# Attention stage of a two-layer streaming encoder: key pairs on column halves, scores in one burst, tile halves fixed by hand, opening in half products

## The chip, the cores and the metric

The kernel runs on one core of a Trainium2 chip, in fp32 and in fp32r (fp32 split into a high and a low part, so that one product is three matmuls: high by high, high by low, low by high). The metric is the time of one execution on the device in microseconds (us). The kernel before takes 2203.91 us, the median of three runs that lie between 2200.82 and 2206.71.

## The reference

One step of a two-layer encoder over 2048 prompt tokens and 32 sample tokens, with a model width of 1024. Layer one is a gated DeltaNet (projections, short convolution, a recurrence in blocks of 64, a gate, an output projection, LayerNorm). From its result `h` a shared K and V are projected, and layer two is attention over a window of the query's own chunk of 64 keys and the two chunks before it, with 16 query heads on 4 key heads of 64 and a learned sink for each head. The change lies in layer two:

```python
def sink_softmax(s, sinks):
    sk = sinks.astype(jnp.float32)[..., None, None]
    m = jnp.maximum(s.max(-1, keepdims=True), sk)
    p = jnp.exp(s - m)
    return p / (p.sum(-1, keepdims=True) + jnp.exp(sk - m))
...
    q = rope_partial(proj[..., :B_QW].reshape(b, l, B_Q_HEADS, B_HD), pos) * (B_HD ** -0.5)
    z = proj[..., B_QW:]
    o = cached_attention(q, k, v, sk) if cached else banded_attention(q, k, v, sk)
    out = (o * jax.nn.silu(z)) @ w_out
    return layer_norm(DN_ALPHA * x + out, ln_g, ln_b)
```

The prompt is 32 chunks of 64 tokens. Chunk n sees the keys of chunks n-2, n-1 and n, 192 keys (chunk 0 sees 64, chunk 1 sees 128). The 32 sample tokens see 128 cached keys and their own 32.

## The kernel before, in words

**Stages.** `P1` projects q, k, v and the gate of layer one; `Delta` runs the recurrence; `O1` makes the output projection and LayerNorm of layer one; `P2` projects V, K, Q and Z of layer two from `h`; `Attention` makes scores, softmax, values, the gate, the output projection and LayerNorm of layer two.

**P2.** Tokens are taken in blocks of 416. Block 0 (phase 0) is projected plainly: a unit is a kind (v, k, q or z) and a number j, it is 256 output columns, and it takes four products (`plain`, L1319). One product is 12 matmuls of 128x416 (L1291 to L1293). The other blocks go in two pairs (phases 1 and 2) by a Winograd scheme of seven products a unit (`winograd`, L1336) on sums of the inputs, which `load_pair` (L1205) makes on VectorE (DVE in the profile) and ScalarE (ACT). The weights of a product are one piece of 512 KB; a ring of 12 pieces holds them, and each product calls for the next loads on ACT's DMA queue (`load`, L1266). After each product up to two pieces of finishing work are taken from a list (`after`, L1304): for q and k a rotation of four DVE operations (`rope`, L1420), for z a tanh on ACT and one DVE operation (`gate`, L1400), for v four transposes and two ACT copies (`turn`, L1406). `sequence` (L1737) sets the order of the units: z0, z1, z2 of phase 0; ten units of phase 1; z3, k0, q0 of phase 0; ten units of phase 2; q1, q2, q3, v0 of phase 0. Six products of the first group lie in stage O1, six beside `load_pair(1)` (L1758); the twelve of z3, k0, q0 lie beside `load_pair(2)` (L1763). The last sixteen products lie in the attention stage, four ahead of each of the chunks 10 to 13 (L1772 to L1776).

**Attention.** Chunks go in the order 10 to 31, then 0 to 9, then the sample. `chunk(n)` (L1610) does two head pairs p, one after the other, and each is a chain of steps: four fp32 score matmuls of 64 rows into `S` (L1624), row maxima on DVE (L1499), four exponentials with row sums on ACT (L1507), one over the sum on DVE (L1510, L1511), scaling of `P` on GpSimd (POOL, L1632), six transposes (L1639) in two groups of three, whose results ACT (L1641) and DVE (L1643) copy, three fp32 value matmuls of 128 rows by 128 columns and 256 moving columns into `ot` (L1645), and the gate (L1648). For the value matmul each chunk of 64 keys stands twice in `vd`, in a block-diagonal form: 128 rows hold the keys for two heads, half of every block is zero. An fp32 matmul is two MATMUL records in the trace, a transpose is one.

Two finished chunks make a tile of 128 tokens. `finish` (L1514) makes its output projection: two halves of 512 columns of 24 matmuls each (L1532 to L1534), then the residual, the statistics (L1535 to L1538), `rsqrt_power` on POOL (L466, L468), the scaling by ACT and POOL (L1543 to L1545) and the store (L1553). There are 17 tiles, the sample's among them. The output weights are 16 pieces of 512 KB, loaded by SP's queue (L999) once P2's memory is free (`open_right`, L1466).

**What sets the order.** Stages before attention are under `manual_schedule`: the order of PE, DVE and ACT is the order of the code. The attention stage is not: there the compiler's planner orders all engines by a simulated time. The queues of SP and POOL are ordered by the planner in both kernels.

Of the kernel before, what the change touches and what calls it, by code (L numbers as in the profile page):

```python
# [19 lines left out]
D = 1024  # L20
NP = 2048
# [1113 lines left out]
class P2:  # L1135
# [10 lines left out]
    def __init__(self, tc, right, mid, I, O, T, G):  # L1146
        self.tc, self.nc, self.I, self.O, self.T, self.G = tc, tc.nc, I, O, T, G
        self.res = new_pool(tc, right, "p2_res", 1, side="right")
        self.wp = new_pool(tc, right, "p2_w", self.RING, side="right")
# [3 lines left out]
        self.ppl = None  # L1153
        self.turn = 0
        self.todo, self.second, self.staged = [], [], []
# [110 lines left out]
    def load(self, most=2):  # L1266

        for _ in range(most):
            if self.loads and len(self.held) < self.RING:
                what, slot = self.loads.pop(0)  # L1270
                w = self.wp.tile([128, 2, 4, 128], F32R, tag="w", name="w")
                src = self.T["w2"][UNITS.index(what[:2]), SLOTS.index(slot)]
                self.nc.scalar.dma_start(w[:].rearrange("p s k c -> p s (k c)").bitcast(F32), src)
# [13 lines left out]
    def product(self, ps, w, x, first, last):  # L1287
        nc = self.nc
        for k in range(4):
# [5 lines left out]
    def units(self, units):  # L1295

        self.loads = [(u, s) for u in units for s in self.slots(u)]
        self.held = []
# [20 lines left out]
    def plain(self, unit):  # L1319
# [3 lines left out]
        for c in range(2):  # L1323
            ps = (self.ppl or self.ppr).tile([128, 512], F32, tag="ps", name="ps")[:, :TB]
            for h in range(2):
                self.product(ps, self.weight(unit, self.PLAIN[c][h]), x[4 * h:4 * h + 4], h == 0, h == 1)
# [111 lines left out]
class Attention:  # L1438


    def __init__(self, tc, left, I, O, T, G):
# [6 lines left out]
        self.ps_s = [new_pool(tc, left, "t_ps", 1, PSUM, side=L)]  # L1448
        self.ps_t = new_pool(tc, left, "t_pt", 2, PSUM, side=L)
        self.ps_o = new_pool(tc, left, "t_po", 1, PSUM, side=L)  # L1450
        self.turn = 0
        self.kT = one.tile([128, 2, NP], F32, tag="kT", name="kT")

        self.vd = one.tile([128, 32, 2, 128], F32, tag="vd", name="vd")
        self.nsk = one.tile([128, 8], F32, tag="nsk", name="nsk")
# [7 lines left out]
        self.pend = []  # L1463
        self.data = {}

    def open_right(self, right):  # L1466
        tc, I = self.tc, self.I
        R = "right"
        self.oone = new_pool(tc, right, "u_one", 1, side=R)
        self.otwo = new_pool(tc, right, "u_two", 2, side=R)  # L1470
        self.pp = new_pool(tc, right, "u_pp", 1, PSUM, side=R)
        self.ps_s.append(new_pool(tc, right, "u_ps", 1, PSUM, side=R))
        rest = load_out_weights(self.nc, self.oone, self.T["wo"][1], self.nc.sync)
        self.w = next(rest)
        drain(rest)

    def tables(self):
        self.tabs = ln_tables(self.nc, self.oone, self.I["b_ln_g"], self.I["b_ln_b"])

    def load_kv(self, a, z):  # L1480
        nc, T = self.nc, self.T
        nc.sync.dma_start(self.kT[:, :, a * 64:z * 64], T["bk"][:, :, a * 64:z * 64].rearrange("a p t -> p a t"))
# [7 lines left out]
    def scores_tile(self):  # L1490
        self.turn += 1
        return self.ps_s[self.turn % len(self.ps_s)].tile([128, 2, 2, 256], F32, tag="S", name="S")

    def softmax(self, S, P, nskc):

        nc, V, thr = self.nc, self.nc.vector, self.thr
        nsub = len(P)
        nm = thr.tile([128, 4], F32, tag="nm", name="nm")
        V.tensor_reduce(out=nm[:, :nsub], in_=S, axis=AX.X, op=ALU.max, negate=True)  # L1499
        V.tensor_tensor(out=nm[:, :nsub], in0=nm[:, :nsub], in1=nskc, op=ALU.min)  # L1500
        sm = thr.tile([128, 4], F32, tag="sm", name="sm")
        es_ = thr.tile([128, 4], F32, tag="es", name="es")
        for u in range(nsub):
            src = S[:, u, :]
            if len(P[u].shape) == 3:
                src = src.rearrange("r (j k) -> r j k", k=64)
            nc.scalar.activation(P[u], src, AF.Exp, bias=nm[:, u:u + 1], scale=1.0, accum_out=sm[:, u:u + 1])  # L1507
        V.tensor_tensor(out=es_[:, :nsub], in0=nm[:, :nsub], in1=nskc, op=ALU.subtract)
        nc.scalar.activation(es_[:, :nsub], es_[:, :nsub], AF.Exp)
        V.tensor_tensor(out=sm[:, :nsub], in0=sm[:, :nsub], in1=es_[:, :nsub], op=ALU.add)  # L1510
        V.reciprocal(out=sm[:, :nsub], in_=sm[:, :nsub])  # L1511
        return sm

    def finish(self, t0, n, graw, late=False, tail=False):  # L1514
        nc, V, pool = self.nc, self.nc.vector, self.otwo
# [5 lines left out]
        nc.gpsimd.tensor_tensor(out=glo[:, :, :n], in0=graw[:, :, :n], in1=ghi[:, :, :n], op=ALU.subtract)  # L1521
        st = pool.tile([128, 2, 6], F32, tag="st", name="st")
        w, tabs = self.w, self.tabs
        both = self.scores_tile() if late else None
        for c in range(2):
            cs = slice(c * 512, c * 512 + 512)
            if late:
# [3 lines left out]
            for k in range(KC):  # L1531
                nc.tensor.matmul(ps[:n], ghi[:, k, :n], w[0][k][:, cs], start=(k == 0), stop=False)  # L1532
                nc.tensor.matmul(ps[:n], ghi[:, k, :n], w[1][k][:, cs], start=False, stop=False)  # L1533
                nc.tensor.matmul(ps[:n], glo[:, k, :n], w[0][k][:, cs], start=False, stop=(k == KC - 1))  # L1534
            V.scalar_tensor_tensor(out=r[:n, cs], in0=r[:n, cs], scalar=ALPHA, in1=ps[:n], op0=ALU.mult, op1=ALU.add)  # L1535
            V.bn_stats(out=st[:n, c, :], in_=r[:n, cs])
# [399 lines left out]
```

## Time and profile before

| what | value |
|---|---|
| median of three runs | 2203.91 us |
| the profiled execution's own time | 2203.02 us |
| its span, first to last instruction | 2201.2 us |
| mean granted TensorE clock | 0.987 |
| DVE, ACT, POOL busy | 68%, 41%, 32% of the span |
| DMA moved | 430 MB, mean 195 GB/s |

The page gives busy times, the span in 40 slices, the DMA queues, the chain of work that ended last, and groups of instructions by line. The trace behind it can be asked for a stretch (the windows view), for instructions in order of time (the timeline view), and for waits. Matmuls are pipelined in it, so a matmul's own duration is longer than its share of TensorE's time; the time from one start to the next is what counts. An entry such as "x6 1.46" is six records whose joint stretch is 1.46 us. PEclk is the granted TensorE clock, 1.00 being full.

### The profile page before, as it was taken

The numbers are of one execution on the slowest core, as the hardware profiler recorded it, in microseconds if no ns is written. First come the engines' busy times: TensorE is split into PE (matmuls) and PEld (weight loads), VectorE is DVE, ScalarE is ACT, GpSimd is POOL, SyncE is SP. The second block draws the span as 40 slices with busy tenths as digits, with TensorE's granted clock in tenths as the row PEclk, the third lists the DMA queues.
The fourth block names the chain that finished last, engine by engine and source line by source line (L and its number), as shares of the span: only waits on it lengthen the run. The fifth ranks groups of instructions, "written<-read, shape, count | busy, mean of one in ns | idle before, by whom it ended". The sixth has DMA issues, their size and how long they took to land.

```text
span 2201.2 us, 37188 instructions
## 1 busy us (share of the span) xinstructions
PE 2103.0 (96%) x13370; PEld 1911.1 (87%) x13370; DVE 1490.1 (68%) x2771; ACT 911.1 (41%) x2405; POOL 713.5 (32%) x1176
## 2 busy tenths in 40 slices
PE   8999999999989999998889999899899988999997
PEld 6999999999989889887778888899899976888775
DVE  5888977876657589888865665555835566556663
ACT  5545545544422477667742111311311034444441
POOL 1212211161111188788841210000000025565653
PEclk9999999999999999999999999999999999999999
DMA  7656656567764645545735766888788895333321
GB/s 283 224 186 192 223 172 195 175 191 242 243 212 161 204 131 163 153 147 180 235 105 179 255 218 243 298 278 284 266 285 285 273 305 135 100 83 96 96 73 43
DMA packets 348377, 430.00 MB, mean 195 GB/s; under 512 B 78352, under 2 KB 276080, under 8 KB 348176
## 3 DMA queue, kind: packets, MB, share of 16 engines
q1 hardware_dynamic: 311856, 311.07, 44.5%
q10 hardware_dynamic: 36336, 116.55, 15.8%
q8 instruction: 106, 1.74, 0.3%
q14 instruction: 79, 0.65, 0.1%
HBM read 269.45 MB, written 158.44 MB: 194 GB/s over the span
## 4 chain that ended last, share of the span: by engine, by line
PE 77%; DVE 9%; POOL 5%; ACT 4%; DMA 3%; issue 2%; ACTq 0%; SPq 0%; POOLq 0%; DVEq 0%
PE ps L77 10%; PE ps L79 10%; PE ps L78 10%; PE ps L1291 5%; PE ps L1292 5%; PE ps L1293 5%; PE ot L1645 3%; PE po L1052 3%; PE po L1054 3%; PE po L1053 3%; PE po L1532 3%; PE po L1533 3%; PE po L1534 3%; PE S L1624 2%; POOL Tt L588 2%
## 5 line engine op out<-in xcount | busy, mean ns | idle before, releaser
L77 PE MATMUL ps<-act_hi,w_hi 128*128 128x416 f32 x1280 | 458.7, 358 | 6.4 <-DVE z L322 2.7
L79 PE MATMUL ps<-act_hi,w_lo 128*128 128x416 f32 x1280 | 450.5, 353 | 5.0 <-POOL w_lo L54 3.2
L78 PE MATMUL ps<-act_lo,w_hi 128*128 128x416 f32 x1280 | 451.3, 353 | 0.0
L77 PEld LDWEIGHTS ps<-act_hi,w_hi 128*128 128x128 f32 x1280 | 241.8, 189 | 11.0 <-DVE z L322 3.1
L79 PEld LDWEIGHTS ps<-act_hi,w_lo 128*128 128x128 f32 x1280 | 242.0, 189 | 9.8 <-POOL w_lo L54 4.3
L78 PEld LDWEIGHTS ps<-act_lo,w_hi 128*128 128x128 f32 x1280 | 242.6, 190 | 2.8
L1291 PE MATMUL ps<-xs_h,w 128*128 128x416 f32 x560 | 199.6, 356 | 11.4 <-DVE ra L1348 7.1
L1292 PE MATMUL ps<-xs_l,w 128*128 128x416 f32 x560 | 199.9, 357 | 3.1 <-DVE xs_l L1194 3.1
L1293 PE MATMUL ps<-xs_h,w 128*128 128x416 f32 x560 | 198.4, 354 | 0.0
L54 POOL TENSOR_TENSOR w_lo<-w_raw,w_hi 128x1024 fp32r<-128x1024 f32 x32 | 80.5, 2516 | 357.3 <-ACT w_hi L53 343.3
L295 DVE SCALAR_TENSOR_TENSOR y<-R,convw,y 128x2083 f32<-128x2083 f32 (+2 forms) x78 | 175.1, 2245 | 24.8 <-ACT y L293 24.6
L585 POOL TENSOR_TENSOR tm<-L,Tt 128x60 f32<-128x60 f32 (+19 forms) x375 | 136.3, 363 | 87.9 <-DVE L L572 49.9
L588 POOL TENSOR_TENSOR Tt<-Tt,tm 128x60 f32<-128x60 f32 (+19 forms) x375 | 143.6, 383 | 28.3
L1632 POOL TENSOR_TENSOR P<-P,sm 128x384 f32<-128x384 f32 (+2 forms) x128 | 100.9, 810 | 119.1 <-DVE sm L1511 56.5
L1486 POOL MEMSET vd<- 64x768 f32 (+2 forms) x10 | 7.8, 778 | 397.0 <-DVE ra L1348 396.7
L1507 ACT ACTIVATE P<-S,nm 128x192 f32<-128x192 f32 (+2 forms) x260 | 104.6, 419 | 61.1 <-DVE nm L1500 52.3
L1291 PEld LDWEIGHTS ps<-xs_h,w 128*128 128x128 f32 x560 | 106.4, 190 | 14.6 <-DVE ra L1348 7.8
L1348 DVE SCALAR_TENSOR_TENSOR ra<-ps,u 128x416 f32<-128x416 f32 x60 | 35.4, 590 | 122.3 <-PE ps L1293 121.4
L1052 PE MATMUL po<-wo,g_hi 128*128 128x512 f32 (+1 forms) x272 | 110.7, 407 | 0.9 <-DVE hT L1100 0.9
L1292 PEld LDWEIGHTS ps<-xs_l,w 128*128 128x128 f32 x560 | 106.2, 190 | 5.6 <-DVE xs_l L1194 4.2
L1293 PEld LDWEIGHTS ps<-xs_h,w 128*128 128x128 f32 x560 | 106.9, 191 | 1.2
L95 ACT CAST pre_hl<-pre_raw 128x256 fp32r<-128x256 f32 x184 | 65.7, 404 | 101.6 <-DMA pre_raw<-in_b_w_z 25.8
(298 smaller groups left out, 4799.8 us busy)
## 6 DMA issues: line engine op xcount, KB each, us to landing
w<-s_w ACTq DMA_DIRECT2D x180, 512.0 KB, 4.6
s_w<-pre_hl SPq DMA_DIRECT2D x160, 256.0 KB, 2.5
w_raw<-in_w_in SPq DMA_DIRECT2D x32, 512.0 KB, 6.5
s_wo<-pre_hl SPq DMA_DIRECT2D x64, 256.0 KB, 4.1
gb<-s_gcum SPq DMA_DIRECT2D x34, 256.0 KB, 5.2
k<-s_k SPq DMA_DIRECT2D x34, 256.0 KB, 4.0
s_z<-z SPq DMA_DIRECT2D x40, 208.0 KB, 2.1
s_q<-y SPq DMA_DIRECT2D x8, 1024.0 KB, 5.2
```

The lines of the kernel that those rows point to most:

```text
L77: nc.tensor.matmul(ps, hi[:, k, :], xh[:, k, :], start=(k == 0), stop=False)
L78: nc.tensor.matmul(ps, hi[:, k, :], xl[:, k, :], start=False, stop=False)
L79: nc.tensor.matmul(ps, lo[:, k, :], xh[:, k, :], start=False, stop=(k == KC - 1))
L295: self.nc.vector.scalar_tensor_tensor(out=y[:, a:z], in0=R[:, a + j:z + j], scalar=self.convw[:, i, j:j + 1], in1=y[:, a:z], op0=ALU.mult, ...
L585: P.tensor_tensor(out=tm[:n, i0 - k:, :w], in0=L[:n, i0:, j:j + 1].to_broadcast(sh), in1=Tt[:n, j:j + 1, :w].to_broadcast(sh), op=ALU.mult)
L588: P.tensor_tensor(out=Tt[:n, i0:, :w], in0=Tt[:n, i0:, :w], in1=tm[:n, i0 - k:, :w], op=ALU.subtract)
L1052: nc.tensor.matmul(ps[:n], ghi[:, k, :n], w[0][k][:, cs], start=(k == 0), stop=False)
L1291: nc.tensor.matmul(ps, w[:, 0, k], xh[:], start=first and k == 0, stop=False, skip_group_check=True)
L1292: nc.tensor.matmul(ps, w[:, 0, k], xl[:], start=False, stop=False, skip_group_check=True)
L1293: nc.tensor.matmul(ps, w[:, 1, k], xh[:], start=False, stop=last and k == 3, skip_group_check=True)
L1507: nc.scalar.activation(P[u], src, AF.Exp, bias=nm[:, u:u + 1], scale=1.0, accum_out=sm[:, u:u + 1])
L1632: nc.gpsimd.tensor_tensor(out=P[:, u, :nj], in0=P[:, u, :nj], in1=f.unsqueeze(1).unsqueeze(3).to_broadcast([128, nj, 2, 64]), op=ALU.mult)
```

## The change

1. **Values on column halves.** Of the three key chunks of a window, two adjoining ones are a pair of 128 keys (`keys`). For the pair, V stands as it is (`vp`, 128 keys by 256 columns, a second load of V), and each head half is a value matmul of 128 rows by 64 columns whose output goes to one half of the PSUM partitions (`ot[hs, p]`). The single chunk uses `vd` as before, one half of the columns at a time. Three fp32 matmuls of 128 columns for each head pair become four of 64 columns. The six transposes stay six.
2. **Scores in one burst.** Both head pairs' scores of a chunk are made together, and the steps of a chunk are spread over two rounds: `beside(n)` makes the scores and the softmax of chunk n, and the transposes and values of the chunk before it.
3. **Order by hand.** The attention stage is under `manual_schedule` for PE, DVE and ACT. A tile's output projection is cut into eight pieces of six matmuls, and each round takes four, so that a half tile ends just ahead of the values. The next tile's split (`ready`) comes in the fifth piece or after, the scaling of a tile (`scale`) in the third piece of the next tile.
4. **Opening in half products.** The last plain products are yielded by halves (`fine`), and `opening` puts the steps of the chunks 10 to 13 between them, chunk 10's scores after six halves.
5. **Plain products dealt out anew.** z3 goes ahead of phase 1 (ten products beside `load_pair(1)` in place of six), v0 takes z3's place beside `load_pair(2)`, and twelve products are left for the opening in place of sixteen.
6. **Output weights in the ring.** The weight ring outlives P2, and its last 12 loads are the first 12 pieces of the output weights; four are left to load after P2. LayerNorm's tables are loaded then too.
7. **The sample** goes after chunk 31 in place of last, and the last tile's store is cut in two, on two queues.

PSUM is dealt out anew: two score tiles from the start, one transpose tile at first and a second after P2.

```diff
-        for k in range(4):
+        for k in ks:
...
-        self.loads = [(u, s) for u in units for s in self.slots(u)]
+        self.loads = [(u, s) for u in units for s in self.slots(u)] + [(None, i) for i in range(self.RING)]
...
+                for ks in ((0, 1), (2, 3)) if self.fine else (range(4),):
+                    if ks[0] == 2:
+                        yield 1.13
+                    self.product(ps, w, x[4 * h:4 * h + 4], h == 0, h == 1, ks)
...
+                if pair is not None:
+                    for h in range(2):
+                        hs = slice(h * 64, h * 64 + 64)
+                        nc.tensor.matmul(ot[hs, p], self.vp[:, pair, p * 128 + h * 64:p * 128 + h * 64 + 64],
+                                         pt[:, 2 * h:2 * h + 2, :], start=True, stop=one is None)
+                if one is not None:
+                    for h in range(2):
+                        hs = slice(h * 64, h * 64 + 64)
+                        nc.tensor.matmul(ot[hs, p], self.vd[:, one, p, hs], pt[:, 4:6, :],
+                                         start=pair is None, stop=True)
...
+    def opening(self, chunks, wait):
+
+        for _ in range(wait):
+            yield
+        for n in chunks:
+            self.scores(n)
+            self.exps(n, 0)
+            if self.prev is None:
+                self.exps(n, 1)
+                for _ in range(4):
+                    yield
+                self.norm(n, 0)
+                self.norm(n, 1)
+                yield
+            else:
+                for i, step in enumerate(itertools.chain(self.turn(self.prev, 0), self.turn(self.prev, 1))):
+                    if i == 1:
+                        self.exps(n, 1)
+                    yield
+                    if i >= 2:
+                        self.norm(n, i - 2)
+                self.values(self.prev)
+            self.prev = n
+
+    def beside(self, n):
+
+        m, self.prev = self.prev, n
+        if n is not None:
+            self.scores(n)
+            self.exps(n, 0)
+        next(self.out)
+        drain(self.turn(m, 0))
+        if n is not None:
+            self.exps(n, 1)
+            self.norm(n, 0)
+        next(self.out)
+        drain(self.turn(m, 1))
+        if n is not None:
+            self.norm(n, 1)
+        next(self.out)
+        next(self.out)
+        self.values(m)
...
+            for j in self.finish(*got, last):
+                if j == 2:
+                    for f in self.todo:
+                        f()
+                    self.todo = []
+                if j >= 4 and ahead is None and self.pend:
+                    ahead = self.ready()
+                yield
...
-    sequence = [("z", j, 0) for j in range(3)] + [p + (1,) for p in pairs]
-    sequence += [("z", 3, 0), ("k", 0, 0), ("q", 0, 0)] + [p + (2,) for p in pairs]
-    sequence += [("q", j, 0) for j in range(1, 4)] + [("v", 0, 0)]
+    sequence = [("z", j, 0) for j in range(4)] + [p + (1,) for p in pairs]
+    sequence += [("v", 0, 0), ("k", 0, 0), ("q", 0, 0)] + [p + (2,) for p in pairs]
+    sequence += [("q", j, 0) for j in range(1, 4)]
...
-        both(itertools.islice(late, 6), p2.load_pair(1))
+        both(itertools.islice(late, 10), p2.load_pair(1))
...
+    order = list(range(10, 32)) + ["s"] + list(range(10))
+    p2.fine = True
+    with tc.manual_schedule(engines={ET.PE, ET.DVE, ET.Activation}):
+        att.load_k(8, 14)
+        att.start(10)
+        att.sinks()
+        for a, z in ((14, 18), (18, 24), (24, 32)):
+            att.load_v(a - (6 if a == 14 else 0), z)
+            att.load_k(a, z)
+        for _ in att.opening([order.pop(0) for _ in range(4)], 6):
+            drain(itertools.islice(late, 1))
+        drain(late)
+        p2.rest()
+        right.close()
+        att.open_right(right, p2.out)
+        att.load_k(0, 8)
+        att.load_v(0, 8)
+        for n in order:
+            att.beside(n)
+        att.rest()
```

`scores` makes both head pairs' `S`, then for each the maxima (L1499, L1500) and the difference to the sink (L1508); `exps` is one head pair's exponentials on ACT; `norm` is one over the sum on DVE and two POOL scalings, of the pair and of the single chunk; `turn` is three transposes with an ACT copy, then three with a DVE copy, each a yield; `values` is the value matmuls of both head pairs and the gate.

More of the change, by code (lines that the diff above doesn't have):

```diff
@@ new lines, in turn @@
+    def turn(self, n, p):
+        nc, V, thr, ident = self.nc, self.nc.vector, self.thr, self.G["ident"]
+        P, single = self.probs.pop((n, p))
+        pt = thr.tile([128, 6, 128], F32, tag="pt", name="pt")
+        self.turned[n, p] = pt
+        if n == "s":
+            for half in range(2):
+                tr = self.turn_tile()
+                nc.tensor.transpose(tr[:, 0, :], P[:, half, 0:128], ident[:, :])
+                nc.tensor.transpose(tr[:32, 1, :], P[:, half, 128:160], ident[:, :])
+                nc.scalar.copy(pt[:, 2 * half, :], tr[:, 0, :])
+                V.tensor_copy(pt[:32, 2 * half + 1, :], tr[:32, 1, :])
+                yield
+            return
+        _, _, pair, at, one, _ = self.keys(n)
+        src = []
+        if pair is not None:
+            src += [(c, P[:, c, at:at + 128]) for c in range(4)]
+        if one is not None:
+            src += [(4 + u, single[:, u].rearrange("r h k -> r (h k)")) for u in range(2)]
+        for copy in (nc.scalar.copy, V.tensor_copy):
+            now, src = src[:3], src[3:]
+            if now:
+                tr = self.turn_tile()
+                for i, (_, a) in enumerate(now):
+                    nc.tensor.transpose(tr[:, i, :], a, ident[:, :])
+                c = now[0][0]
+                copy(pt[:, c:c + len(now), :], tr[:, :len(now), :])
+            yield
@@ L1516, in finish, with ready @@
+    def ready(self):
+        nc, pool = self.nc, self.otwo
+        t0, n, graw = self.pend.pop(0)
         r = pool.tile([128, D], F32, tag="r", name="r")
@@ L1521, in finish, with outs @@
         nc.gpsimd.tensor_tensor(out=glo[:, :, :n], in0=graw[:, :, :n], in1=ghi[:, :, :n], op=ALU.subtract)
+        return t0, n, r, ghi, glo
+    def outs(self):
+        got = self.ready()
+        while got is not None:
+            ahead = None
+            last = self.late and not self.pend
+            for j in self.finish(*got, last):
+                if j == 2:
+                    for f in self.todo:
+                        f()
+                    self.todo = []
+                if j >= 4 and ahead is None and self.pend:
+                    ahead = self.ready()
+                yield
+            got = ahead
+    def finish(self, t0, n, r, ghi, glo, tail):
+        nc, V, pool = self.nc, self.nc.vector, self.otwo
         st = pool.tile([128, 2, 6], F32, tag="st", name="st")
         w, tabs = self.w, self.tabs
-        both = self.scores_tile() if late else None
+        both = self.scores_tile() if self.late else None
         for c in range(2):
             cs = slice(c * 512, c * 512 + 512)
-            if late:
+            if both is not None:
                 ps = both[:, c].rearrange("p u k -> p (u k)")
@@ L1545, in finish @@
             nc.gpsimd.tensor_tensor(out=r[:n], in0=r[:n], in1=tabs[1][:n], op=ALU.add)
-        else:
-            for c in range(2):
-                cs = slice(c * 512, c * 512 + 512)
+            nc.sync.dma_start(self.O["y"][t0:t0 + n, :], r[:n])
+        if not tail:
+            self.todo.append(scale)
+        else:
+            halves = [slice(c * 512, c * 512 + 512) for c in range(2)]
+            for cs in halves:
                 V.scalar_tensor_tensor(out=r[:n, cs], in0=r[:n, cs], scalar=mv[:n, 0:1], in1=tabs[0][:n, cs],
@@ L1652, in flush @@
-    def flush(self, keep):
-        while len(self.pend) > keep:
-            self.finish(*self.pend.pop(0), late=(keep == 0), tail=(keep == 0 and len(self.pend) == 0))
+                queue.dma_start(self.O["y"][t0:t0 + n, cs], r[:n, cs])
+        yield 7
 class Filler:
@@ L1747, in program @@
     right.close()
-    p2.append(P2(tc, right, mid, I, O, T, G))
+    ring = ExitStack()
+    p2.append(P2(tc, ring, right, mid, I, O, T, G))
     o1[0].room = p2[0].spare
```

336 lines of the change are left out of this document (173 added, 163 removed).

## The prediction, made before the result was known

> **What bounds the kernel now.** I read the page's head first, then the stretches of the last two stages, then the order of the instructions on PE inside one chunk, then the chain of waits where PE had gaps.
>
> ```profile
> span 2201.2 us, 37188 instructions
> PE 2103.0 (96%) x13370; PEld 1911.1 (87%) x13370; DVE 1490.1 (68%) x2771; ACT 911.1 (41%) x2405; POOL 713.5 (32%) x1176
> ```
>
> PE is the busy engine, and no other comes near it. So the sum is one of PE time: records taken away, and stretches in which PE stands still. The profiled execution took 2203.02 us, 1.8 more than its span and 0.9 under the median of 2203.91; the sum is made on 2203.0.
>
> The windows view (columns: stretch, then busy time and records of PE, weight loads, DVE, ACT, POOL, then granted clock, DMA share and GB/s) shows where PE stands still:
>
> ```profile
> 1380.00:1400.00 20.00, 12.24 (x44) 9.65 (x43) 16.21 (x32) 10.28 (x22) 0.00 (x0) 0.74 0.86 286
> 1587.00:1594.00 7.00, 0.42 (x3) 0.07 (x1) 6.02 (x14) 0.00 (x0) 0.00 (x0) 0.73 0.97 355
> 1790.00:1830.00 40.00, 28.94 (x185) 20.81 (x182) 23.96 (x58) 20.48 (x87) 12.31 (x16) 1.00 1.05 327
> 1847.25:1916.33 69.08, 69.08 (x385) 55.57 (x385) 39.58 (x102) 33.54 (x126) 42.86 (x40) 1.00 0.30 84
> ```
>
> The first two are the starts of P2's pairs, where inputs are not made yet; the third is the opening of attention, with DMA full; the fourth is steady attention, where PE never rests while POOL is busy 62% of the time, DVE 57%, ACT 49%. The last window is six chunks long: from the value matmuls of one chunk to those of the sixth after it, 69.08 / 6 = 11.51 us a chunk.
>
> **The chunk on PE.** In the timeline (start, joint stretch, engine, line, count) the difference of starts gives the price of one record:
>
> ```profile
> 1902.13 0.40 PE L1534 MATMUL po<-wo,g_lo 128*128 128x512 f32 x1
> 1904.42 0.39 PE L1532 MATMUL po<-wo,g_hi 128*128 128x512 f32 x1
> 1904.66 1.46 PE L1645 MATMUL ot<-pt,vd 128*128 128x256 f32 x6
> 1905.95 0.82 PE L1639 MATMUL tr<-ident,P 128*128 128x128 f32 x6
> 1906.70 0.92 PE L1624 MATMUL S<-kT,qs 64*128 64x192 f32 x8
> 1907.55 0.50 PE L1533 MATMUL po<-wo,g_hi 128*128 128x512 f32 x1
> 1911.69 0.60 PE L1639 MATMUL tr<-ident,P 128*128 128x128 f32 x4
> ```
>
> An output matmul is (1904.42 - 1902.13) / 10 = 0.229 us. Six value records take 1905.95 - 1904.66 = 1.29, 0.215 each. Two transposes more cost 0.82 - 0.60, so 0.11 each. Score records have 192 columns, at the values' rate 0.161 each; eight in a row would be 1.29, but the burst is over in 0.85, so the two row halves run together: four steps of 0.161 are 0.64. The other 0.21, and 0.10 between the last transpose (1905.95 + 6 x 0.11 = 1906.6) and the burst, are the switch into halves and out: 0.31 a burst. A chunk is then 2 x (0.64 + 0.31 + 0.66 + 1.29 + 12 x 0.229) = 11.3, and 11.5 is measured: the prices are right.
>
> **Values on column halves.** Twelve value records a chunk become sixteen of the same 256 columns. If two column halves run together, they are eight steps of 0.215: 4 x 0.215 = 0.86 less a chunk, for the chunks 1 to 31 (chunk 0 stays) -26.7 us. No row of before has 128-row matmuls on both column halves. The nearest has 64 rows, where two halves of the columns share the rows with different moving data:
>
> ```profile
> 771.09 0.68 PE L696 MATMUL bps<-ta,npr 64*64 64x64 f32 x16
> 771.71 0.66 PE L612 MATMUL vtr<-ident,v 128*128 128x128 f32 x4
> ```
>
> Sixteen records of 64 columns (0.054 each at the values' rate, 0.86 in a row) are over in 0.62 with a switch at each end; eight steps of 0.054 are 0.43, which leaves 0.19 for the switches. They overlapped: a pair took 1.0 steps if the switches cost that 0.19, and 1.44 (0.62 / 0.43) if they cost nothing. I take 1.0, since the switches of the score bursts cost more than 0.19; no overlap at all is a rival. The Trainium skill, "TensorE: Matmul & The Clock Gate", Part 3, states that three matmuls of 32 columns side by side went 2.38 times as fast as in turn, not three times. By that rate a pair of halves would take 1.26 steps, and the sum would come out some 14 us higher. The 64-row records lie nearer to 1.0, so the sum stays.
>
> **Scores in one burst.** Scores, transposes and output records stay as many. Now a chunk enters and leaves halves twice, four switches at 0.155; after, out to values, values to scores, scores to out are three. -0.155 x 32 = -5.0 us; 0 if the switch between the two kinds of halves costs two, -10 if a whole burst's 0.31 goes.
>
> **Order by hand in the round.** The work of other engines per chunk stays; what counts is whether the fixed order makes PE wait. The rows that decide:
>
> ```profile
> 1902.51 1.07 ACT L1520 CAST g_hi<-graw 128x1024 fp32r<-128x1024 f32 x1
> 1904.60 0.21 ACT L1509 ACTIVATE es<-es 128x4 f32<-128x4 f32 x1
> 1904.97 2.37 POOL L1521 TENSOR_TENSOR g_lo<-graw,g_hi 128x1024 fp32r<-128x1024 f32 x1
> 1906.53 0.48 ACT L1641 COPY pt<-tr 128x384 f32<-128x384 f32 x1 [1.72 <-PE tr L1639]
> 1906.91 0.43 ACT L1507 ACTIVATE P<-S,nm 128x192 f32<-128x192 f32 x1
> 1907.31 0.42 ACT L1507 ACTIVATE P<-S,nm 128x192 f32<-128x192 f32 x1
> 1907.66 0.96 DVE L1499 TENSOR_REDUCE nm<-S 128x4 f32<-128x768 f32 x1 [0.30 <-PE S L1624]
> ```
>
> From the start of a burst: the first head pair is done at 0.9, its maxima at 2.2 (0.30 and 0.96), its four exponentials (0.40 apart) and the sink's at 4.0, and only then can ACT copy the first transposes, until 4.5. PE comes back to that transpose tile after scores (1.5), a piece (6 x 0.229 = 1.37), six transposes (0.66) and another piece, at 4.9. It holds, by 0.4. In every second round `ready` puts g_hi (1.07) on ACT ahead of that copy: the copy ends at 5.6 and PE waits 0.7, in 15 rounds 10 us. These times are good to half a microsecond either way, so I take +6, from 0 to +12. Everything else has a round of slack: P is scaled (POOL) a whole round before it is transposed, and the copies of the second transposes end 2 us ahead of the values. The round is then 1.29 + 12 x 0.11 + 1.72 + 5.50 + 0.46 = 10.3, and with the 0.2 that the sum of before left open 10.5, with the wait 10.7.
>
> **Plain products dealt out anew.** P2's matmuls start 0.19 apart:
>
> ```profile
> 1757.50 0.36 PE L1292 MATMUL ps<-xs_l,w 128*128 128x416 f32 x1
> 1757.69 0.35 PE L1293 MATMUL ps<-xs_h,w 128*128 128x416 f32 x1
> ```
>
> In the window at 1380, 44 records are 8.4 us of work, so 11.6 us are lost there, the lowered clock (0.74) among it. Four more products (48 x 0.19 = 9.1 us) now lie ahead while `load_pair(1)` goes on, but z3 adds two operations of its own on DVE, which is busy 16.2 of those 20 us. I take -9 (0 if DVE sets the end, -11 at most). At 1587 PE stands for 7 us while DVE works; v0 in place of z3 takes two operations off DVE there: -1 (+1 if its copies delay ACT, -2).
>
> **Opening.** The chain of waits, with the loads:
>
> ```profile
> 1803.22 0.94 PE S L1624 x8
> 1807.80 0.95 PE S L1624 x8
> 1812.38 0.94 PE S L1624 x8
> 1825.81 3.88 DMA qs<-s_bq
> 1830.52 2.36 POOL g_lo L1521
> ```
>
> Before, once P2 is out of work, a head pair takes 4.58 us where its records take 0.95 + 0.66 + 1.29 = 2.90. Five such stretches lose 8 us, and the waits for q and the first tile's split some 6 more: 14 lost. After, this work lies between P2's products and the output weights are in the ring, so those waits go; others come, because PE's order is fixed:
>
> ```profile
> 1765.12 0.39 SPq L1482 DMA_DIRECT2D kT<-s_bk  x1
> 1768.94 0.80 SPq L1605 DMA_DIRECT2D qs<-s_bq  x1
> kT<-s_bk SPq DMA_DIRECT2D x2, 512.0 KB, 6.4
> ```
>
> K for chunk 10 goes out 7.4 us after the last Winograd matmul (1757.69) and takes about 6.4 to land, behind it q; the scores are due after six halves, 6 x 6 x 0.19 = 6.9 us. I count 6 us of waiting (0 to 10: SP has fewer loads ahead of q now). With one transpose tile until P2 is gone, PE needs ACT's copy back after 1.5 us and gets it some 1.5 us later, in three chunks: 5. The first tile has nothing ahead of it: its g_hi comes after the exponentials (5.1), g_lo at 7.5, PE is there at 1.5: 6. Small waits: 1. That is 18 against 14: +4, from -9 to +20.
>
> **Tail.** The end of the chain:
>
> ```profile
> 2167.43 0.43 PE S L1532
> 2167.86 0.43 PE S L1533
> 2189.68 2.41 POOL r L1544
> 2192.16 2.33 POOL r L1545
> 2194.49 0.63 POOL ln_y L466
> ```
>
> After the sample's short matmuls PE goes 0.43 a record, not 0.229, for about ten: 2 us that go when the sample stands in the middle. The last tile's POOL step waits behind the scaling of the tile before it; that scaling now starts in the last tile's third piece, seven microseconds earlier: about 2.5. -4.5 (-2 to -6).
>
> **Sum.** -26.7 - 5.0 + 6 - 9 - 1 + 4 - 4.5 = -36.2, and 2203.0 - 36.2 = 2166.8: 2167 us. The bounds of the unknown terms, added as squares (5, 6, 9, 2, 16, 2 upward; 5, 6, 2, 1, 13, 2 downward), give 20 up and 15 down: 2152 to 2187 for this case alone, chance 0.61.
>
> **The rivals.**
>
> *Halves overlap in part.* At the middle of what the 64-row records allow, a pair takes 1.22 steps: 0.22 x 8 x 0.215 x 31 = +12, 2179. For it: full-height halves move twice the data. Chance 0.06. The rate that the Trainium skill states (above) is of this kind.
>
> *The opening starves.* From the end of P2's pairs to the first tile, K (1.5 MB), V twice (3), q and z (2 to 3), 16 pieces of output weights (8.4) and tables (1) are due, some 17 MB; at the 327 GB/s of the third window 52 us, against about 46 us of PE work there. SP's queue is in order, and one K or V load ahead of a due q holds PE for several microseconds. Some 20 us more: 2187. For it: DMA share 1.05 already. Against: PE's waiting itself gives the queues time. Chance 0.14.
>
> *Another engine sets the round.* If the hand-made order ties ACT, DVE and POOL into one chain, the round stays near 11.5 in 28 rounds, +1.0 each with the wait taken off: about +26, 2193. Against: POOL has 42.9 of 69, and would have 68% of a 10.5 us round. Chance 0.08; together with a starved opening, where nothing but P2's and the tail's gain is left and lost again, about 2203, no change: 0.04.
>
> *Slower: the halves run in turn.* Then sixteen records of 0.215 follow each other, eight steps more than forecast: 8 x 0.215 x 31 = +53, 2220. It decides once about two thirds (36 of 53) of the overlap is lost. For it: two streams of 128 rows each have to enter the same rows, which nothing in this trace does; the sample's 128-row halves go one at a time. Against: the 64-row records above. Chance 0.07.
>
> **How the numbers follow.** Faster takes the forecast and the first three rivals, 0.61 + 0.06 + 0.14 + 0.08 = 0.89; same 0.04; slower 0.07. The bound between them is 0.3%, 6.6 us, about what a measurement of this kernel can tell from no change. The range 2148 to 2193 leaves out the slower case, the unchanged one and a few hundredths at either end of the others.
>
> **What would show it.** Right: value records on the two halves starting at nearly one time, eight steps of 0.215 a chunk; rounds of 10.4 to 10.8; no PE gap of over 2 us near 1390, one of 6 near 1590; a wait of several microseconds ahead of chunk 10's scores; and in every second round a PE wait on ACT's copy. Wrong: value records 0.215 apart one by one (a round of 12.2), PE waiting for DMA in the opening for more than 15 us, or rounds of 11.5 with PE idle in them.

## The result, and the profile after

The changed kernel takes 2233.51 us in the median (2231.09 to 2239.82, four runs) where the kernel before takes 2202.36 on the same chip: ratio 1.0143, 95% interval 1.0124 to 1.0161. It is 31 us slower; 2167 had been forecast. The lines below answer to those of the prediction. First the head of the page of the changed kernel:

```profile
span 2229.3 us, 37382 instructions
PE 2078.9 (93%) x13494; PEld 1874.6 (84%) x13494; DVE 1463.2 (66%) x2769; ACT 907.0 (41%) x2405; POOL 714.1 (32%) x1170
```

PE has 24.1 us less work than before (2078.9 against 2103.0), though its span is 28.1 us longer: some 52 us of standing still are new. The windows view shows where they are not, and where they are (columns as in the prediction):

```profile
1380.00:1400.00 20.00, 15.72 (x79) 14.54 (x78) 14.65 (x29) 9.88 (x21) 0.00 (x0) 0.99 0.84 293
1757.00:1850.00 93.00, 58.60 (x322) 47.61 (x322) 42.18 (x109) 24.84 (x105) 24.77 (x28) 0.80 0.91 244
1850.00:1992.00 142.00, 127.96 (x813) 94.41 (x812) 77.02 (x201) 62.85 (x251) 79.83 (x76) 1.00 0.31 87
```

The start of P2's first pair (first row) is better: 79 records in 20 us where there were 44, at a clock of 0.99 in place of 0.74. A wait of 3.1 us is left there, and the slow matmuls that follow it begin at 1399.8, so that this row does not show them. The opening (second row) has PE at work for 63% of the time. And the steady rounds (third row) leave PE idle for 14 of 142 us, where the kernel before left it no idle time at all. The waits view of the steady stretch from 1850 to 2000 (what PE waited for: us in all, times, longest) names the wait:

```profile
PE ot L1672 <- DVE graw L1681: 13.1, 13, 1.1
PE tr L1648 <- ACT pt L1650: 1.8, 6, 0.3
```

The second row is the wait for ACT's copy in every second round, which was forecast. The first comes in every round (30.4 us in 31 times over the whole stage) and was not. The timeline of one round's end shows how it arises (start, joint stretch, engine, line):

```profile
1958.39 0.39 PE L1778 MATMUL po<-wo,g_lo 128*128 128x512 f32 x1
...
1958.71 0.65 PE L1672 MATMUL ot<-pt,vp 128*64 128x256 f32 x4
1958.82 0.69 DVE L1781 SCALAR_TENSOR_TENSOR r<-r,po 128x512 f32<-128x512 f32 x1 [1.50 <-PE po L1778]
...
1959.19 0.60 PE L1677 MATMUL ot<-pt,vd 128*64 128x256 f32 x4
1959.54 0.69 DVE L1782 BATCH_NORM_STATS2 st<-r 128x6 f32<-128x512 f32 x1
1960.27 0.21 DVE L1786 BATCH_NORM_AGGREGATE mv<-st 128x2 f32<-128x12 f32 x1
1960.39 0.38 DVE L1681 TENSOR_TENSOR graw<-ot,zs 128x256 f32<-128x256 f32 x1
...
1960.91 0.65 PE L1672 MATMUL ot<-pt,vp 128*64 128x256 f32 x4 [1.12 <-DVE graw L1681]
1961.37 0.63 PE L1677 MATMUL ot<-pt,vd 128*64 128x256 f32 x4
```

Two things are to be read here. The first four value records of a head pair start within 0.48 us (1958.71 to 1959.19), two steps of 0.24 and not four: the column halves run side by side (single records start in pairs 7 ns apart). And the second head pair, due two steps after 1959.19, begins at 1960.91: its first matmul waits for the gate of the first head pair, since both write and read the one tile `ot`. That gate is 0.38 long, but it stands on DVE behind the residual (0.69) and the statistics (0.69 and 0.21) of the half tile whose last matmul came just ahead of the values. This work makes about half of the wait: the gate needs the first pair's values, whose last record ends at 1959.79, and it starts at 1960.39.

The opening, by the waits view from 1750 to 1850:

```profile
PE S L1575 <- DMA qs<-s_bq: 9.3, 1, 9.3
PE tr L1648 <- ACT pt L1650: 8.3, 3, 5.7
PE tr L1648 <- POOL P L1605: 8.1, 1, 8.1
PE po L1776 <- ACT g_hi L1744: 5.8, 1, 5.8
PE ot L1672 <- DVE graw L1681: 1.6, 3, 0.6
PE po L1778 <- POOL g_lo L1745: 1.2, 1, 1.2
```

These are 34.3 us; the same view of the kernel before has 12.7, none of them for a load:

```profile
PE S L1624 <- ACT P L1507: 8.8, 7, 2.4
PE tr L1639 <- POOL P L1632: 1.9, 6, 0.6
PE ot L1645 <- ACT pt L1641: 1.7, 2, 1.5
PE po L1534 <- POOL g_lo L1521: 0.3, 1, 0.3
```

In the changed kernel's view the fifth row prices the gate by itself: in the opening no half tile ends ahead of the values, and the wait is at most 0.6. The chain of its second and third rows leads to ACT. Its timeline there (ACTq is its queue of loads; the bracket is the time that it stood, and what ended it):

```profile
1785.34 0.33 ACTq L1275 DMA_DIRECT2D w<-s_wo  x1
1785.71 0.52 ACT L1340 ACTIVATE a<-ps 128x416 f32<-128x416 f32 x1 [5.09 <-DMA vd<-s_bv]
...
1799.63 0.33 ACTq L1275 DMA_DIRECT2D w<-s_wo  x1
1800.01 0.52 ACT L1340 ACTIVATE a<-ps 128x416 f32<-128x416 f32 x1 [8.13 <-DMA kT<-s_bk]
```

Ahead of each of ACT's copies of a finished product stands the issue of an output-weight load, and that issue waits until a load of V or of K that SP's queue made has landed. Behind ACT's copy waits DVE's rotation (15.5 us in three waits), behind that the rest of DVE and POOL, and in the end PE's transposes.

Where the time went, by stages (starts of the named matmuls in the two traces, in us):

| stretch | before | changed |
|---|---|---|
| O1's last matmul to P2's last Winograd matmul | 402.5, 302 plain matmuls in it | 407.4, 348 plain matmuls in it |
| to the 13th output matmul | 80.7 | 88.2 |
| to the last matmul | 353.0 | 372.5 |
| to the end | 9.9 | 8.6 |

The 46 plain matmuls that moved from the second stretch to the first are 46 x 0.19 = 8.7 us. The kernel before also makes two chunks' scores, one chunk's transposes and a chunk and a half of values more ahead of its 13th output matmul, about 7 us at the prices of the changed kernel's round (an estimate). With both taken into account P2 gained 3.8, the opening lost 7.5 + 8.7 + 7 = 23, the rounds lost 19.5 - 7 = 12.5, or 14.5 without the 2 us that the tail's slow records gave back (records behind the last values now start 0.23 apart at once), and the end gained 1.3. That is a loss of some 30.5 us; the span grew by only 28.1, since the changed trace comes to O1's end 2.5 us earlier, in code that is the same: that point lies between 1347 and 1360 us in the traces of this study.

### The profile page after: what moved, and what is told of

It is laid out like the page before. It is cut to its first block, busy times and chain, and to the rows that moved or that the text cites. A ratio compares the mean times of both kernels' runs of the same rounds, so it can differ in the third digit from the quotient of the medians.

```text
span 2229.3 us, 37382 instructions
## 1 busy us (share of the span) xinstructions
PE 2078.9 (93%) x13494; PEld 1874.6 (84%) x13494; DVE 1463.2 (66%) x2769; ACT 907.0 (41%) x2405; POOL 714.1 (32%) x1170
## 5 line engine op out<-in xcount | busy, mean ns | idle before, releaser
L1605 POOL TENSOR_TENSOR P<-P,sm 128x512 f32<-128x512 f32 (+2 forms) x126 | 100.9, 824 | 140.7 <-DVE sm L1602 98.9
L1508 POOL MEMSET vd<- 64x1024 f32 (+2 forms) x8 | 7.6, 947 | 401.8 <-DVE ra L1358 401.6
L1054 PE MATMUL po<-wo,g_lo 128*128 128x512 f32 (+1 forms) x272 | 106.4, 391 | 0.0
```

## The experiments

Times are medians; the ratio is always to the kernel before on the same chip, and differences between experiments are differences of these ratios by 2202 us.

**Both gates behind both head pairs' values.** The changed kernel, with this in `values`:

```diff
+        gates = []
         for p in range(2):
...
-            V.tensor_tensor(out=graw[:, p * 4:p * 4 + 4, sl], in0=of, in1=zs[:, p * 4:p * 4 + 4, sl], op=ALU.mult)
+            gates.append((p, of))
+        for p, of in gates:
+            V.tensor_tensor(out=graw[:, p * 4:p * 4 + 4, sl], in0=of, in1=zs[:, p * 4:p * 4 + 4, sl], op=ALU.mult)
```

> The changed kernel, with both head pairs' value matmuls of a chunk ahead of both gates. Theory A (PE waits in every round, because the second head pair's values come into the PSUM tile that DVE's gate of the first pair is still reading): the gap of 1.3 to 1.5 us between the two groups of value matmuls shrinks to a step of 0.21, 1.2 us in each of 30 rounds, 36 us: about 2195 (2189 to 2202). Theory B (the gap belongs to the column halves themselves, a drain ahead of a new group): no change, about 2231. Theory C (the wait only moves to another place of the round): 2215 to 2231.

2202.36 us, ratio 1.0001 (0.9986 to 1.0016): 31 us less than the changed kernel. The waits of PE from 1850 to 2000, all of them, and the starts of four score bursts:

```profile
PE tr L1648 <- ACT pt L1650: 6.7, 7, 1.1
```

```profile
1890.96 1.57 PE L1575 MATMUL S<-kT,qs 64*128 64x192 f32 x16
...
1902.66 1.57 PE L1575 MATMUL S<-kT,qs 64*128 64x192 f32 x16
...
1913.09 1.57 PE L1575 MATMUL S<-kT,qs 64*128 64x192 f32 x16
...
1924.79 1.57 PE L1575 MATMUL S<-kT,qs 64*128 64x192 f32 x16
```

The wait for the gate is gone and the rounds are 10.43 and 11.70 in turn. Two adjoining rounds of the changed kernel took 23.86 (1938.07 to 1961.93). Every second round is the forecast round; in the other the wait for ACT's copy has grown from 0.3 to 1.1, since PE now comes back to the transposes that much sooner. So by the rounds the removal gives 0.86 a round (11.93 against 11.07 in the mean), less than the 1.0 that the wait cost. The loss of the changed kernel against the kernel before is as large as this one wait; without it the two are level.

**The next tile's split one piece later**, in the changed kernel and in the one above:

```diff
-                if j >= 4 and ahead is None and self.pend:
+                if j >= 5 and ahead is None and self.pend:
```

> Kernel: the changed one with nothing but the next tile's split moved from the fifth piece to the sixth; the gates stay between the two head pairs' values. Theory A (the wait for the gate comes every round and stands by itself, the wait for ACT's copy of 0.71 comes in every second round beside it): -0.71 x 16 = -11, so 2222, and rounds of 11.6. Rival K (the two waits cover each other, since PE stands for whichever is later): 0 to -3, so 2231 to 2234, rounds of 11.9.

> As e1_gates_last, and the next tile's split (g_hi on ACT) one piece later, behind ACT's exponentials of the second head pair. Theory A (the 0.7 us gap ahead of the second transposes in every second round is ACT's copy waiting behind g_hi): 0.6 us in 14 rounds less than e1_gates_last, some 8 us, about 2187. Theory C (ACT is then late for the second transposes' copy, and the values wait): equal to e1_gates_last within 3 us.

In the changed kernel: 2220.06 us, ratio 1.0080 (1.0050 to 1.0110), 14 less. With the gates last: 2189.11, ratio 0.9936 (0.9919 to 0.9953), 14 less as well. By the rounds of the traces the first gain is smaller, 11.93 to 11.68 in the mean, some 7 us; the second is 11.07 to 10.59, 13 us. The times alone can't tell 7 from 14, as the two ratios of the first gain are each uncertain by 2 to 3 thousandths, 4 to 7 us. By the rounds the two waits cover each other in part, and neither goes away with the other. The burst starts with both changes:

```profile
1896.80 1.57 PE L1575 MATMUL S<-kT,qs 64*128 64x192 f32 x16
...
1907.54 1.57 PE L1575 MATMUL S<-kT,qs 64*128 64x192 f32 x16
...
1917.98 1.57 PE L1575 MATMUL S<-kT,qs 64*128 64x192 f32 x16
...
1928.72 1.57 PE L1575 MATMUL S<-kT,qs 64*128 64x192 f32 x16
```

10.74 and 10.44 in turn, 10.59 in the mean.

**Values at full width.** What the column halves are worth, with everything else kept: the value matmuls of 128 columns and the layout of `P` as before, first with the gates last alone, then with the later split as well:

```diff
-                _, _, pair, _, one, _ = self.keys(n)
...
+                for j in range(nj):
+                    nc.tensor.matmul(ot[:, p], self.vd[:, k0 // 64 + j, p, :], pt[:, 2 * j:2 * j + 2, :],
+                                     start=(j == 0), stop=(j == nj - 1))
```

> As e1_gates_last, with the value matmuls as before the change: three of 128 columns for each head pair on the block-diagonal V, P laid out for it. Everything else stays. Theory A (two column halves run at one time, eight steps of 0.215 in place of twelve): 0.86 us a chunk more than e1_gates_last, 27 us, about 2222. Theory B (column halves bring nothing): equal to e1_gates_last. If half the overlap were lost: 13 us more.

> Kernel: the one with both gates after both head pairs' values and the next tile's split in the sixth piece, with the value matmuls at full width as before (and P laid out for them). Against the same kernel on column halves (2189.1 us) only the value matmuls differ, and here no longer wait on ACT eats the difference. Theory A (two column halves overlap fully, eight steps of 0.215 a chunk in place of twelve, 0.86 a round in 31 rounds): +27, so 2216, rounds of 11.45. Rival I (the halves gain only what the other run showed, 0.35 a round in the mean, since another engine sets the rest): +11, so 2200, rounds of 10.95.

2213.02 us, ratio 1.0047 (1.0029 to 1.0065), 10 more than with the halves; and 2203.91, ratio 1.0011 (0.9998 to 1.0025), 16 more. In the first, rounds of 11.16 and 11.67 stand against 10.43 and 11.70: in every second one the halves gain nothing, since ACT's copy sets it. The second falls between its two expectations, 27 for a full overlap and 11 for what the first had shown. Its rounds say why:

```profile
1903.53 2.75 PE L1668 MATMUL ot<-pt,vd 128*128 128x256 f32 x12
1906.21 1.57 PE L1575 MATMUL S<-kT,qs 64*128 64x192 f32 x16
...
1914.69 2.75 PE L1668 MATMUL ot<-pt,vd 128*128 128x256 f32 x12
1917.37 1.57 PE L1575 MATMUL S<-kT,qs 64*128 64x192 f32 x16
```

Every round is 11.16 and PE waits for nothing. With the halves a round without a wait is 10.44, so they are worth 0.72: the 0.86 of four steps saved, less about one switch of the array. In every second round 0.3 of that goes into the wait for ACT's copy, because PE now comes sooner than the copy. That leaves 0.57 a round, or 16 in 28 rounds. Against the 11.51 of the kernel before, the 11.16 also show that one burst in place of two and the order by hand are together worth 0.35 a round; no run separates them.

**The new deal of the plain products alone**, in the kernel before, and the old deal in the best kernel below:

```diff
-    sequence = [("z", j, 0) for j in range(3)] + [p + (1,) for p in pairs]
-    sequence += [("z", 3, 0), ("k", 0, 0), ("q", 0, 0)] + [p + (2,) for p in pairs]
-    sequence += [("q", j, 0) for j in range(1, 4)] + [("v", 0, 0)]
+    sequence = [("z", j, 0) for j in range(4)] + [p + (1,) for p in pairs]
+    sequence += [("v", 0, 0), ("k", 0, 0), ("q", 0, 0)] + [p + (2,) for p in pairs]
+    sequence += [("q", j, 0) for j in range(1, 4)]
...
-        both(itertools.islice(late, 6), p2.load_pair(1))
+        both(itertools.islice(late, 10), p2.load_pair(1))
...
-        drain(itertools.islice(late, 4))
+        drain(itertools.islice(late, 3))
```

> The kernel before, with only the plain products dealt out anew (z3 ahead of phase 1, v0 in z3's place, twelve products left for the opening). The forecast's term: 10 us faster, 2192. Theory A (DVE's making of the inputs sets the end, so little is gained): 3 to 5 us faster, about 2198. Theory C (the products that leave the opening uncover its loads): no change or slower.

> Kernel: the one with both gates last, the split in the sixth piece and the ring's output weights on SP's queue (2182.9 us), with the plain products dealt as in the kernel before: six beside the first pair's loads, z3 beside the second's, sixteen left for the opening. Theory A (the new deal gains what the trace of the changed kernel shows in P2, some 4 us, and four products more in the opening cover little of its waits): +4, so 2187. Rival J (the products taken out of the opening are what the opening lacks: eight more half products cover up to 8 us of waits for K and q): -5, so 2178. Forecast of the prediction: the new deal is worth 10, so +10, 2193.

Alone: 2214.72 us, ratio 1.0055 (1.0040 to 1.0070), 12 slower. Of the three expectations only theory C allowed this, but its reason, loads that the missing products no longer cover, is not what the trace shows: no wait of PE from 1755 to 1850 is for a load. P2 itself did gain 3 (its stretch took 408.8 with 350 plain matmuls in it, and 48 x 0.19 = 9.1 of work had moved there), but the planner laid the attention stage out anew around the missing products: the 13th output matmul comes at 1816.2 in place of 1838.3, and from there to the last matmul it is 389.1 in place of 353.0. So this run prices the planner's order and not the deal. Under the order by hand it can be priced: the old deal gives 2189.17, ratio 0.9944 (0.9923 to 0.9964), 6 slower than the new one beside it (0.9917, 0.9898 to 0.9936, the next experiment). The intervals overlap, so the times alone allow 0 to 12; the stretches of the two traces put 4 of the difference in P2 and 2 in the opening. The new deal is worth about 6, by this, and not 10.

**Output weights on SP's queue.** The kernel with both waits taken away, and:

```diff
-                    self.nc.scalar.dma_start(flat.bitcast(F32), self.T["wo"][1][slot // 2, :, slot % 2])
+                    self.nc.sync.dma_start(flat.bitcast(F32), self.T["wo"][1][slot // 2, :, slot % 2])
```

> As e2_split_later (2189), with the twelve ring loads of output weights issued on SP's queue, not on ACT's. Theory D (in the opening ACT stands for 5 and 8 us in front of two ring loads, each of which waits on a semaphore that a K or V load of SP's queue still holds; exponentials, copies and the rotation's inputs queue behind): the two PE gaps of 8.2 and 6.3 us go down to 3 or less, 8 to 12 us less, about 2179. Theory E (DMA is full, and the gaps come from data): no change. Theory F (SP's queue, in order, gets longer, so q of a later chunk comes late): equal or slower by up to 8.

2182.91 us, ratio 0.9917 (0.9898 to 0.9936): 0.8% under the kernel before, no version of the study has a lower ratio, and it is 4 (by the ratios) to 6 (by the medians) less than with the loads on ACT's queue. The intervals of the two overlap; in the traces the stretch from P2's last Winograd matmul to the 13th output matmul falls from 87.6 to 79.8. The waits of the opening, from 1755 to 1850:

```profile
PE S L1575 <- DMA qs<-s_bq: 15.2, 2, 9.1
PE po L1779 <- ACT g_hi L1747: 5.7, 1, 5.7
PE tr L1648 <- POOL P L1605: 2.9, 1, 2.9
PE tr L1648 <- ACT pt L1650: 1.3, 1, 1.3
PE po L1781 <- POOL g_lo L1748: 1.2, 1, 1.2
```

The waits behind ACT fell from 9.3 and 7.9 in the same kernel with the loads on ACT's queue to 1.3 and 2.9. But a second wait for q has come (6.1). The output weights that now stand ahead of chunk 12's q on SP's queue did not make that q late: by the semaphore events it lands at 1799.96, and at 1800.74 in the changed kernel, where P2's last Winograd matmul starts within 0.3 us of the same time. PE comes to chunk 12's scores sooner, at 1800.0 in place of 1808.3, and meets a wait that was hidden before. Half of what was won went there.

**Three tries at the first wait for q.** The sinks loaded first (DVE stands 8.85 us behind that load in the changed kernel), the scores after twelve halves in place of six (`opening(..., 12)`), and, in one kernel, the output weights on SP's queue, the sinks first and ten halves:

> As e2_split_later (2189), with the prompt's sinks loaded ahead of K and q (two loads in front), the sample's sinks loaded later. Theory G (DVE stands 9 us for the sinks' loads, and the first maxima and a rotation queue behind it): the maxima of chunk 10 start some 4 us earlier and the 8.2 us gap shrinks by as much; K and q come 1 us later: 3 us less, about 2186. Theory D (that gap hangs on ACT's ring load): no change, or 1 us slower.

> As e2_split_later (2189), chunk 10's scores after twelve half products in place of six. Theory H (PE reaches these scores before q has landed because the planner puts the first six halves ahead of phase 2's last products, so they cover nothing): the gap of 9.4 to 10 us shrinks to about 3, and the later steps of the opening lack the six halves that were moved: 3 to 7 us less in all, about 2184. Rival (total work and the chain of chunks set the end, not this gap): no change.

> As e2_split_later (2189), with all three: ring loads on SP, sinks first, ten halves ahead of chunk 10. If the theories D, G and H hold and add up: 2170 to 2176. If the opening is bound by DMA: 2186 to 2192.

2193.09 (ratio 0.9958, 0.9940 to 0.9976), 2198.34 (0.9990, 0.9979 to 1.0001) and 2182.07 (0.9919, 0.9900 to 0.9937). The first two are slower than the kernel with both waits taken away (0.9936), by 5, where the intervals still overlap, and by 12. With the sinks first, the wait for q stayed at 9.9 and the one for POOL's scaling grew from 7.9 to 14.3; with twelve halves, the wait for q fell to 4.7, and the waits for ACT's copies grew from 9.3 to 24.1. The third is no better than the output weights on SP's queue alone: the waits for q fell from 15.2 to 13.1, and 4.7 us came up for output weights that had not landed. Each of these moves a wait to the next place in a chain of loads. What would shorten the chain was not found.

## Why the prediction was wrong

**The step that failed** is the sentence "Everything else has a round of slack". The prediction followed the scores, the exponentials, the copies and the split through a round, but not the gate. `values` had been described as "the value matmuls of both head pairs and the gate"; the code has a gate after each pair. Before, the two pairs' values lay half a chunk apart, so the gate of one was long over when the other wrote `ot`. Brought together, they wait for each other, and the half tiles that end just ahead put 1.4 to 1.6 us of DVE work in front of the gate. That is 1.0 us of waiting in each of 31 rounds by the waits view: 0.5 to 0.6 that the gate costs in the opening too, with nothing in front of it, and 0.3 to 0.5 for the work in front. The first experiment, with the gates moved and nothing else, is faster by 31 us, and the wait is gone from its trace. This one wait made the kernel slower. Without it the kernel is level with the one before, and still 35 from the forecast; by the stretches of that trace 17 of these lie in the opening, 11 in the rounds (the wait for ACT's copy), 7 in P2 and 1 in the tail. None of the rivals held it: the nearest, "another engine sets the round", argued from POOL's busy time, and that its price of 26 us was close is luck; an engine with time to spare can still hold PE up by the place of one instruction in its order.

**Values on column halves (forecast -26.7), scores in one burst (-5).** The mechanism was right and so was the sum of the two: 0.86 + 0.16 = 1.02 a round was forecast, and a round without waits went from 11.51 to 10.44, 1.07 less. The parts were divided a little differently: the burst, with the order by hand in it, is worth 0.35 and the halves 0.72. The rival on which the slower case hung, halves that run in turn, fell; so did the partial overlap. The Trainium skill's rate for three tiles of 32 columns ("TensorE: Matmul & The Clock Gate", Part 3), 2.38 in place of 3, does not carry over: two halves of 64 columns took a step each pair.

**The wait for ACT's copy (+6).** It comes in every second round as described, and the split one piece later takes all but 0.3 of it away: 7 us by the rounds and 14 by the times in the changed kernel, 13 and 14 in the kernel with the gates last. The place was right; the cost was twice the value taken, at or above the upper bound of 12, once PE came to the transposes without the other wait ahead.

**Plain products (-10).** 4 to 5 in P2's own stretch, 6 by the old deal. The waits at its two starts went from 14.5 to 7.7 us, and a new one of 1.5 came, ahead of v's transposes. DVE still sets the end at both places, with 3.1 at the first; the lines of the second:

```profile
PE ps L1297 <- DVE ra L1358: 3.4, 1, 3.4
PE ps L1423 <- ACT a L1340: 1.5, 1, 1.5
```

(Waits of the changed kernel from 1564 to 1610; the kernel before waited 6.7 where the first line has 3.4.)

**Opening (+4).** It lost about 23. The 14 us of waits of the kernel before were 12.7; the 18 of the changed one were 34.3. The 6 for the first tile were 5.8 and 1.2, and the 6 for q were 9.3, within its bounds. The six halves that were to cover q had been put ahead of P2's last Winograd products by the planner in the kernel before already (326 of 480 plain matmuls lie ahead there, 372 now), so nothing lay between. What the prediction did not have at all is ACT's queue: it had costed the ring's loads at nothing, as bytes, and not as instructions that stand in front of ACT's other work. The experiment that moves them shows that cost. It did not ask either what a long wait does to the clock (below). The rival "the opening starves" was right in size, with 20 us more, but only in part in kind: of the 34.3 us that PE waited, 9.3 were for a load, and most of the others came by way of ACT.

**Tail (-4.5).** 1.3 at the end and the 2 of the slow records: -3.3.

**The sum**, for the kernel of the study that has the two waits and ACT's queue mended, by the same stretches: P2 -4.6, opening about +15, rounds -26.7, tail -3.3, together -19.6; its span is 21.3 under the one before, 1.5 of it ahead of O1's end. The rounds come within 1 of the forecast's -25.7, but in part by luck: the forecast held +6 for a wait of which this kernel has only 0.3 in every second round, and without it would be -31.7. What keeps this kernel from 2167 is the opening (11) and P2 (5).

## What to carry to other kernels

When steps that lay far apart are brought together, go through every tile that they share, and for each wait through all that is queued ahead of the releasing instruction on its engine: a 0.38 us gate cost 1.0 us a round, half of it because both head pairs share one tile and up to half because of 1.4 us of work in front of it, on an engine that was busy for two thirds of the time. A load that is moved to another queue is an instruction on the engine that issues it: ask what it may have to wait for, and what stands behind it. And a part of a change that is tried alone under a planner that orders the rest is not priced by that, as the deal of products showed: +12 alone, -6 in place.

## What the runs showed of the hardware

**The issue of a load can hold up its engine for another queue's load.** ACT stood 5.1 and 8.1 us at two output-weight loads. The trace's semaphore events show each of these waiting for a semaphore that had been given to a load of SP's queue still on its way: the last event of that load lies at 1785.26 and at 1799.56, and ACT goes on at 1785.28 and 1799.58. With the output weights on SP's queue the same two copies stood for nothing and for 0.29 us; a later copy still stood for 5.3. That it is the shared semaphore, and not the depth of ACT's queue, is read from the trace and was not tried by itself.

**A long wait costs more than its length.** After the 9.3 us ahead of the first scores, the timeline of the changed kernel shows:

```profile
1769.69 2.93 PE L1575 MATMUL S<-kT,qs 64*128 64x192 f32 x16 [9.28 <-DMA qs<-s_bq]
1772.55 0.71 PE L1297 MATMUL ps<-x_h,w 128*128 128x416 f32 x1
...
1774.11 0.55 PE L1298 MATMUL ps<-x_l,w 128*128 128x416 f32 x1
1774.45 0.55 PE L1299 MATMUL ps<-x_h,w 128*128 128x416 f32 x1
1774.80 0.49 PE L1297 MATMUL ps<-x_h,w 128*128 128x416 f32 x1
1775.12 0.35 PE L1298 MATMUL ps<-x_l,w 128*128 128x416 f32 x1
1775.31 0.35 PE L1299 MATMUL ps<-x_h,w 128*128 128x416 f32 x1
```

The burst takes 2.86 in place of 1.50 and the products start 0.35 apart in place of 0.19, until 1775: 5.4 us of work at about half the rate, some 2.6 us lost. The granted clock of the stretch from 1766 to 1775 is 0.50. The same follows the waits of 8.1, 5.7 and 5.8 us: some 10 us in all (an estimate: half of the 5.4, 6.0, 3.2 and 5.2 us that PE worked at the lowered clock). The waits in the opening of the kernel before, 2.4 us at most, leave the clock at 1.00, and so does the wait for the gate in every round. But the waits of 3.1 and 3.4 us at the starts of P2's pairs do not: some 1 to 1.5 us after PE has gone on, its matmuls start 0.35 apart for some 3 us (1399.8 to 1402.9 and 1597.9 to 1601.0). The Trainium skill has the rule ("TensorE: Matmul & The Clock Gate", Part 1): half the clock after about 3.4 us of idling, and as long of steady work to have it back. The traces agree roughly with the first, as waits of 2.4 us left the clock whole and waits of 3.1 us and more did not; for the second they show 3.2 to 6.5 us after the four waits of the opening.

**Two column halves with different moving data lose nothing.** Pairs of value records start 7 ns apart, a step each 0.215 us for 256 columns of fp32, with 128 rows each; only the switch into the halves and out of them is paid (0.14 a round more than at full width, 0.86 less 0.72).
